# A gated DeltaNet's chunk preparation by pairs of directions, with inverse steps on 32 new rows and beta inside the block inverses

## The chip, the cores and the metric

The kernel runs on one core of one Trainium2 chip. The metric is device time in microseconds (us) of one execution. Three runs of the kernel before the change took 1604.45, 1605.53 and 1607.15 us, a median of 1605.53. A separate execution was recorded by the hardware profiler. Engines: TensorE (PE, with PEld for its weight loads), VectorE (DVE), ScalarE (ACT), GpSimd (POOL) and SyncE (SP, which here issues nearly all DMAs).

## The reference

One layer of a diffusion backbone over 1024 latent and 256 context tokens of width 1024: adaptive normalisation, one input projection, two groups of heads (a gated DeltaNet with 4 heads of 128, and neighbourhood attention with 8 heads of 64), an output projection and a SwiGLU network. The change touches only what the DeltaNet computes for each chunk ahead of its scan. Cut to that:

```python
def chunk_gated_delta_rule(q, k, v, g, beta, S0):
    gam = jnp.cumsum(g..., axis=-1)                       # log decay, per chunk
    decay = jnp.exp(jnp.where(tril, gam[..., :, None] - gam[..., None, :], -jnp.inf))
    kb = k * beta[..., None]
    m = jnp.where(strict, einsum("bhncd,bhnmd->bhncm", kb, k) * decay, 0.0)
    a_mat = jnp.eye(CHUNK) + m
    u = triangular_solve(a_mat, v * beta[..., None], lower=True, unit_diagonal=True)
    w = triangular_solve(a_mat, kb * jnp.exp(gam)[..., None], lower=True, unit_diagonal=True)
    qk = jnp.where(tril, einsum("bhncd,bhnmd->bhncm", q, k) * decay, 0.0)
    ...                                                   # then a scan over the chunks
o_f, S_f = chunk_gated_delta_rule(q, k, v, g[0], beta[0], S0_f)
o_b, S_b = chunk_gated_delta_rule(rev(q), rev(k), rev(v), rev(g[1]), rev(beta[1]), S0_b)
```

So for each chunk, head and direction the inverse of a unit triangular matrix is needed, and the masked product of q and k with its decay.

## The kernel before, in words

The kernel works with chunks of 128 tokens: 10 chunks (2 of context, 8 latent), 4 heads, 2 directions d, so 20 cases (d, c). It runs in stages.

1. Modulation and normalisation, then the projection (L970 to L1045). Its work is a list of jobs: blocks of 128 columns (`Block`, kinds k, q, v, nk, nq) and row tiles (`Wide`, kinds z and nv). Each product is done in three parts, high times high, low times high and high times low, all from L397 or L580.
2. Beside the projection, `Background` generators put other work between its products. `bg` holds first `block_inverses` (L781), which inverts the 32x32 diagonal blocks of all 80 matrices, and then `preps` (L870), which makes the 128x128 inverses. `bg2` holds the sums of the modulation. Between two k steps of a block `bg.step` advances that work, by 1 step up to the job number `turn` and by 3 after it (L1030); between row tiles by 2 and by 5 (L1022, L1024). Latent chunks can only be prepared when the q blocks are done. What is left is drained ahead of the last block, nq 3 (L999).
3. The scan over the chunks in both directions (L1112), with neighbourhood attention (L247) put between its products, then the output projection and the SwiGLU network.

The order that each engine's queue has in the end is made by a scheduler in the language's tile layer, by its own costs and the dependencies; it moves instructions against the order in which the code issues them.

Preparation of one case (`prep`, L896): POOL makes two tiles `rg` (L903), ACT and POOL lay the 32x32 blocks from the DMA tile `xc` on the diagonals of `fx` and `x0` (L908, L909). PE sums the decays (L913, L914), ACT takes the exponential (L917), DVE multiplies `kk` by it and by -beta, head by head (L919), and for latent chunks `at` by the exponential (L923). PE multiplies by the diagonal blocks (L928), ACT copies that to `f` (L930). Three steps then extend the inverse from the diagonal: PE multiplies all 128 rows by `f` (L937) and DVE adds `x0` (L938). Up to three cases are alive at once, each one stage further at a time, and the products go through two PSUM banks named `pr`. SP loads `kk`, `xc` and `at` (L888, L889, L893), and stores `y` and `am` through the list `stores` (L947). After the last case the attention's pool takes over the memory, and its loads (L253 to L276) follow on SP.

`block_inverses` ends by writing U and its blockwise transpose to `x_d` (L858 to L864).

Of the kernel before, what the change touches and what calls it, by code (L numbers as in the profile page):

```python
# [9 lines left out]
F32 = mybir.dt.float32  # L10
F32R = mybir.dt.float32r
# [3 lines left out]
OP = mybir.AluOpType  # L15
# [72 lines left out]
def hybrid(ctx, tc, a, dbg):  # L88
# [280 lines left out]
    with ExitStack() as bs:  # L369
# [411 lines left out]
        def block_inverses():  # L781
            with ExitStack() as gs:
# [75 lines left out]
                for d in range(2):  # L858
                    ud = U[:, d * NU:(d + 1) * NU]
                    ut = g4.tile([128, NU, 32], F32, name="ut", tag="ut")  # L860
                    dve.transpose(fl(ut), fl(ud))
# [8 lines left out]
        def preps():  # L870

            first_half.close()
            with ExitStack() as gs:
                pk = pools(gs, "pk", "left")
                shift(gs, "ppad", "left", 64)
                pp = pools(gs, "pp", "left")

                def work(name, bufs=2, dt=F32):
                    return (pk if name == "kk" else pp).tile([128, 4, 128], dt, name=name, tag=name, bufs=bufs)

                x0s, fxs = [[work(f"{m}{i}", 1) for i in range(k)] for m, k in (("x0", 3), ("fx", 2))]
                for t in x0s + fxs:
                    pool.memset(t, 0.0)

                def fetch(d, c):

                    kk, xc = work("kk", 4), pp.tile([128, 2, 4, 32], F32, name="xc", tag="xc", bufs=2)
                    sp.dma_start(kk, kk_d[:, c])  # L888
                    sp.dma_start(xc, x_d[:, d, :, c * 4:c * 4 + 4])  # L889
                    at = None  # L890
                    if c >= 2:
                        at = work("at", 2)
                        sp.dma_start(at, qk_d[:, c - 2])  # L893
                    return d, c, kk, xc, at

                def prep(n, d, c, kk, xc, at):  # L896
                    lat = c >= 2
                    mle = M[C_LE + d].rearrange("p (o i) -> p o i", o=1).to_broadcast([128, 4, 128])
                    rgs = []
                    for gg in (GH, GL):  # L900
                        rg = work("rg", 2, F32R)
                        src = gg.bitcast(F32)[:, d, c].rearrange("p (h o) -> p h o", o=1).to_broadcast([128, 4, 128])
                        pool.tensor_tensor(rg, src, mle, OP.mult)  # L903
                        rgs.append(rg)
                    x0, fx = x0s[n % 3], fxs[n % 2]
                    for b in range(4):
                        q = slice(b * 32, b * 32 + 32)
                        act.copy(fx[q, :, q], xc[q, 1])  # L908
                        pool.tensor_copy(x0[q, :, q], xc[q, 0])  # L909
                    yield 1  # L910
                    p = bank("pr")
                    for j, rg in enumerate(rgs):
                        pe.matmul(p, mr[:, d], fl(rg), start=j == 0, stop=False)  # L913
                    pe.matmul(p, mr[:, 4], mneg[:, d].rearrange("p (o i) -> p o i", o=1).to_broadcast([128, 4, 128]),  # L914
                              start=False, stop=True)
                    e = work("y", 4)
                    act.activation(fl(e), p, AF.Exp)  # L917
                    for h in range(4):
                        dve.scalar_tensor_tensor(kk[:, h], kk[:, h], NB[:, d, c, h:h + 1], e[:, h],  # L919
                                                 op0=OP.mult, op1=OP.mult)  # L920
# [5 lines left out]
                    p = bank("pr")  # L926
                    for h in range(4):
                        pe.matmul(p[:, hs[h]], kk[:, h], fx[:, h], start=True, stop=True)  # L928
                    f = kk
                    act.copy(fl(f), p)  # L930
                    yield 1
                    y = e
                    src = x0
                    for _ in range(3):
                        p = bank("pr")
                        for h in range(4):
                            pe.matmul(p[:, hs[h]], f[:, h], src[:, h], start=True, stop=True)  # L937
                        dve.tensor_tensor(fl(y), p, fl(x0), OP.add)  # L938
                        src = y
                        yield 1  # L940
                    stores.append((y_d[d, c], y, tick[0] + 2))

                stores, tick = [], [0]

                def flush(n):
                    while stores and stores[0][2] <= n:
                        sp.dma_start(*stores.pop(0)[:2])  # L947

                todo = [(d, ORDER[d][i]) for i in range(NCH) for d in range(2)]
                live, landing = [], []  # L950
                n = 0
                while live or todo or landing:
                    if not landing and todo and (todo[0][1] < 2 or all(x in done for x in queries)):
                        landing.append(fetch(*todo.pop(0)))
# [5 lines left out]
                    nxt = []  # L960
                    for g in live:
                        tick[0] += 1
                        flush(tick[0])
                        if next(g, 0):
                            nxt.append(g)
                        yield
                    live = nxt
                flush(tick[0] + 2)

        jobs = first + [Block("k", 2), Block("k", 3), Wide("z", 1, zp)]  # L970
# [717 lines left out]
```

## Time and profile before

| what | us |
| --- | --- |
| runs, median (lowest to highest) | 1605.53 (1604.45 to 1607.15) |
| span of the profiled execution, first to last instruction | 1601.8 |
| PE busy in it | 1509.9 (94%) |
| DVE busy | 1038.7 (65%) |
| ACT busy | 706.1 (44%) |
| POOL busy | 205.5 (13%) |
| preparation's first and last step products (L937) | 294.5 and 588.9 |
| first score product of the attention (L296) | 623.8 |

The span is the only time that the profile gives for its own execution; the median of the runs is 3.7 us above it. Lines such as L937 are lines of the kernel's file. A group's row gives line, engine, operation, `output<-inputs`, shapes and count, then busy us and the mean ns of one, then the engine's idle time before them and who ended it. Products are pipelined and their ends are modelled: a product's price is best read from the time between two starts. An fp32 product appears as two instructions on PE, each with its own weight load. Releasers are inferred from semaphore events.

### The profile page before, as it was taken

To read this page: it belongs to the slowest core of one execution; us is meant where nothing else is said; L and a number is where in the kernel's file an instruction comes from. 1 tells how busy PE (TensorE), PEld (TensorE's weight loads), DVE (VectorE), ACT (ScalarE), POOL (GpSimd) and SP (SyncE) were. 2 spreads that over 40 slices of the span, in tenths; PEclk is the share of its full clock that TensorE was granted. 3 is DMA by queue.
4 is the path that set the end of the run, shared out by engine and by line. 5 is a ranking of instruction groups with operands and counts; after the bars stand their busy time and mean duration, and the time that the engine had idled before them with its cause. 6 is when DMAs were issued, how large, how long until landed. Compare 5 with 4: busy or idle time off the path is not lost. (4 is left out here: it accounts for less than half of the span.)

```text
span 1601.8 us, 24051 instructions
## 1 busy us (share of the span) xinstructions
PE 1509.9 (94%) x8626; PEld 1269.3 (79%) x8626; DVE 1038.7 (65%) x1934; ACT 706.1 (44%) x1341; POOL 205.5 (13%) x277
## 2 busy tenths in 40 slices
PE   4999999899898897999899999999999999999999
PEld 2788787679788786788777887888888888888887
DVE  4774496674364476667898648956665655679652
ACT  5342554553332325666674347333333333545441
POOL 0054401611333320011110000000000000000000
PEclk8999999999999999999999999999999999999999
DMA  9254222665345538999754910522333333698742
GB/s 387 63 190 133 71 74 78 202 200 178 117 150 184 182 102 228 311 286 288 217 161 135 310 55 27 197 99 99 112 101 107 116 109 109 233 369 299 254 153 85
DMA packets 206407, 271.03 MB, mean 169 GB/s; under 512 B 15952, under 2 KB 115792, under 8 KB 205264
## 3 DMA queue, kind: packets, MB, share of 16 engines
q1 hardware_dynamic: 200816, 264.73, 50.8%
q10 hardware_dynamic: 5472, 4.76, 0.9%
q8 instruction: 68, 1.11, 0.3%
q14 instruction: 51, 0.42, 0.1%
HBM read 204.68 MB, written 68.94 MB: 171 GB/s over the span
## 5 line engine op out<-in xcount | busy, mean ns | idle before, releaser
L397 PE MATMUL blk<-hh,whi 128*128 128x512 f32 (+1 forms) x416 | 125.1, 393 | 4.2 <-ACT hh L702 2.8
L1325 ACT CAST uhi<-ws 128x512 fp32r<-128x512 f32 x91 | 54.7, 622 | 153.8 <-PE ps L1264 75.1
L1325 ACT CAST uhi<-wq 128x512 fp32r<-128x512 f32 x101 | 60.3, 621 | 135.7 <-issue 61.3
L397 PE MATMUL blk<-hh,wlo 128*128 128x512 f32 (+1 forms) x416 | 117.8, 375 | 0.6 <-POOL wlo L194 0.6
L397 PE MATMUL blk<-hl,whi 128*128 128x512 f32 (+1 forms) x416 | 117.5, 374 | 0.0
L1326 DVE TENSOR_TENSOR ulo<-wq,uhi 128x512 fp32r<-128x512 f32 x101 | 67.2, 686 | 66.3 <-ACT uhi L1325 35.4
L1264 PE MATMUL ps<-hT,uhi 128*128 128x512 f32 x336 | 103.9, 390 | 3.1 <-ACT hT L1439 3.1
L1264 PE MATMUL ps<-lT,uhi 128*128 128x512 f32 x336 | 103.9, 391 | 0.0
L1264 PE MATMUL ps<-hT,ulo 128*128 128x512 f32 x336 | 103.8, 390 | 0.0
L1264 PE MATMUL ps<-hB,uhi 128*128 128x512 f32 x288 | 89.7, 392 | 0.0
L1264 PE MATMUL ps<-lB,uhi 128*128 128x512 f32 x288 | 89.2, 391 | 0.0
L1264 PE MATMUL ps<-hB,ulo 128*128 128x512 f32 x288 | 88.9, 389 | 0.0
L397 PEld LDWEIGHTS blk<-hh,whi 128*128 128x128 f32 x416 | 70.8, 194 | 19.7 <-issue 4.9
L397 PEld LDWEIGHTS blk<-hl,whi 128*128 128x128 f32 x416 | 73.5, 192 | 15.2 <-issue 1.7
L397 PEld LDWEIGHTS blk<-hh,wlo 128*128 128x128 f32 x416 | 73.3, 191 | 15.2 <-POOL wlo L194 0.9
L1326 DVE TENSOR_TENSOR ulo<-ws,uhi 128x512 fp32r<-128x512 f32 x91 | 60.7, 685 | 37.7 <-ACT uhi L1325 29.4
L580 PE MATMUL blk<-zhi,hh 128*128 128x256 f32 (+1 forms) x288 | 84.4, 293 | 0.0
L580 PE MATMUL blk<-zhi,hl 128*128 128x256 f32 (+1 forms) x288 | 82.9, 288 | 0.0
L580 PE MATMUL blk<-zlo,hh 128*128 128x256 f32 (+1 forms) x288 | 82.2, 285 | 0.0
L193 ACT CAST whi<-wraw 128x1024 fp32r<-128x1024 f32 x26 | 27.3, 1048 | 112.7 <-PE blk L397 55.7
L1264 PEld LDWEIGHTS ps<-hT,uhi 128*128 128x128 f32 x336 | 62.8, 188 | 16.5 <-ACT hT L1439 3.5
L1264 PEld LDWEIGHTS ps<-hT,ulo 128*128 128x128 f32 x336 | 63.4, 189 | 13.3
(352 smaller groups left out, 3749.0 us busy)
## 6 DMA issues: line engine op xcount, KB each, us to landing
wq<-w_fo SPq DMA_DIRECT2D x99, 256.0 KB
wq<-w_gu SPq DMA_DIRECT2D x88, 256.0 KB
wad<-wa SPq DMA_DIRECT2D x64, 256.0 KB
bt<-rpb SPq DMA_DIRECT2D x64, 192.0 KB
t_d<-g SPq DMA_DIRECT2D x22, 512.0 KB
fr<-t_d SPq DMA_DIRECT2D x44, 256.0 KB
f_d<-g SPq DMA_DIRECT2D x33, 256.0 KB
fr<-f_d SPq DMA_DIRECT2D x33, 256.0 KB
```

Of the source, the lines that this page charges most:

```text
L193: act.copy(h, r)
L397: pe.matmul(o, ww[:, k], xx[k][:, s], start=k == 0 and j == 0, stop=k == KT - 1 and j == 2)
L580: pe.matmul(p[:, :c1 - c0], x[k][:, s], ww[:, k, c0:c1], start=k == 0 and j == 0, stop=k == KT - 1 and j == 2)
L1264: pe.matmul(o, w[wi][:, k], x[xi][:, k], start=first and k == 0 and j == 0, stop=k == n - 1 and j == 2, skip_group_check=True)
L1325: act.copy(hi, self.raw[key])
L1326: dve.tensor_tensor(lo, self.raw[key], hi.bitcast(F32), OP.subtract)
```

## The change

Preparation now takes a pair, both directions of the same step i of the scan order, in one generator, and every stage is issued for d = 0 and d = 1 together.

- `block_inverses` multiplies one of the two stored block forms by NB (which is -beta with the norm of k) on DVE ahead of its store. The diagonal product then carries beta, so the multiplication of `kk` by beta head by head goes, and one elementwise product of 128x512 with the exponential is left.
- The step tile `y` begins with the diagonal blocks. Step n computes only the 32 rows that are new (rows block n for one direction, block 3 - n for the other) over the 32n columns that can be nonzero. The two directions write different groups of 32 PSUM partitions, in two banks, and their products alternate by head. DVE copies the new rows of d = 0, ACT those of d = 1; nothing is added.
- `at` is multiplied in place and stored from there. The tiles' buffer numbers double, six tiles are cleared at the start, not five, and y is stored one tick earlier.
- A second pair may start once the first has passed three stages. The background is advanced by 1 between k steps and by 2 between row tiles, also after `turn`.

The diff:

```diff
@@ block_inverses
                     dve.transpose(fl(ut), fl(ud))
-                    sp.dma_start(x_d[:, d, d], ud)
-                    sp.dma_start(x_d[:, d, 1 - d], ut)
+                    plain, scaled = (ud, ut) if d == 0 else (ut, ud)
+                    sp.dma_start(x_d[:, d, 0], plain)
+                    dve.tensor_tensor(scaled, scaled, NB[:, d].rearrange("p c (h o) -> p (c h) o", o=1).to_broadcast(
+                        [128, NU, 32]), OP.mult)
+                    sp.dma_start(x_d[:, d, 1], scaled)
@@ preps
-                x0s, fxs = [[work(f"{m}{i}", 1) for i in range(k)] for m, k in (("x0", 3), ("fx", 2))]
-                for t in x0s + fxs:
+                fxs = [work(f"fx{d}", 1) for d in range(2)]
+                ys = [[work(f"y{d}{i}", 1) for d in range(2)] for i in range(2)]
+                for t in fxs + ys[0] + ys[1]:
                     pool.memset(t, 0.0)
+                q32 = [slice(b * 32, b * 32 + 32) for b in range(4)]
...
-                def prep(n, d, c, kk, xc, at):
...
+                def prep(i, got):
+                    y = ys[i % 2]
                     rgs = []
...
+                    for d, c, kk, xc, at in got:
+                        for q in q32:
+                            act.copy(fxs[d][q, :, q], xc[q, 1])
                     yield 1
...
-                    for h in range(4):
-                        dve.scalar_tensor_tensor(kk[:, h], kk[:, h], NB[:, d, c, h:h + 1], e[:, h],
-                                                 op0=OP.mult, op1=OP.mult)
-                    if lat:
-                        am = work("am", 3)
-                        dve.tensor_tensor(am, at, e, OP.mult)
-                        stores.append((at_d[d, c - 2], am, tick[0] + 2))
+                    for (d, c, kk, xc, at), e in zip(got, es):
+                        dve.tensor_tensor(kk, kk, e, OP.mult)
+                    for (d, c, kk, xc, at), e in zip(got, es):
+                        for q in q32:
+                            pool.tensor_copy(y[d][q, :, q], xc[q, 0])
+                        if at is not None:
+                            dve.tensor_tensor(at, at, e, OP.mult)
+                            stores.append((at_d[d, c - 2], at, tick[0] + 2))
                     yield 1
...
-                    for _ in range(3):
-                        p = bank("pr")
-                        for h in range(4):
-                            pe.matmul(p[:, hs[h]], f[:, h], src[:, h], start=True, stop=True)
-                        dve.tensor_tensor(fl(y), p, fl(x0), OP.add)
-                        src = y
+                    for n in range(1, 4):
+                        blk = (q32[3 - n], q32[n])
+                        cols = (slice(128 - 32 * n, 128), slice(0, 32 * n))
+                        ps = [bank("pr").rearrange("p (h i) -> p h i", h=4) for _ in got]
+                        for h in range(4):
+                            for (d, c, kk, xc, at), p in zip(got, ps):
+                                pe.matmul(p[blk[d], h, :32 * n], kk[:, h, blk[d]], y[d][:, h, cols[d]],
+                                          start=True, stop=True)
+                        dve.tensor_copy(y[0][blk[0], :, cols[0]], ps[0][blk[0], :, :32 * n])
+                        act.copy(y[1][blk[1], :, cols[1]], ps[1][blk[1], :, :32 * n])
                         yield 1
-                    stores.append((y_d[d, c], y, tick[0] + 2))
+                    for d, c, kk, xc, at in got:
+                        stores.append((y_d[d, c], y[d], tick[0] + 1))
...
-                    if landing and len(live) < 3:
-                        live.append(prep(n, *landing.pop(0)))
-                        n += 1
+                    if landing and (not live or len(live) < 2 and live[0][1] >= 3):
+                        live.append([prep(*landing.pop(0)), 0])
@@ the projection's loop
-                        bg.step(5)
+                        bg.step(2)
...
-                    bg.step(1 if n < turn else 3)
+                    bg.step(1)
```

More of the change, by code (lines that the diff above doesn't have):

```diff
@@ new lines, in preps, with fetch @@
+                q32 = [slice(b * 32, b * 32 + 32) for b in range(4)]
+                def fetch(i):
+                    got = []
+                    for d in range(2):
+                        c = ORDER[d][i]
+                        kk, xc = work("kk", 6), pp.tile([128, 2, 4, 32], F32, name="xc", tag="xc", bufs=4)
+                        sp.dma_start(kk, kk_d[:, c])
+                        sp.dma_start(xc, x_d[:, d, :, c * 4:c * 4 + 4])
+                        at = None
+                        if c >= 2:
+                            at = work("at", 4)
+                            sp.dma_start(at, qk_d[:, c - 2])
+                        got.append((d, c, kk, xc, at))
+                    return i, got
@@ new lines, in prep @@
+                def prep(i, got):
+                    y = ys[i % 2]
+                    rgs = []
+                    for d, c, kk, xc, at in got:
+                        mle = M[C_LE + d].rearrange("p (o i) -> p o i", o=1).to_broadcast([128, 4, 128])
+                        for gg in (GH, GL):
+                            rg = work("rg", 4, F32R)
+                            g = gg.bitcast(F32)[:, d, c].rearrange("p (h o) -> p h o", o=1).to_broadcast([128, 4, 128])
+                            pool.tensor_tensor(rg, g, mle, OP.mult)
+                            rgs.append(rg)
+                    for d, c, kk, xc, at in got:
+                        for q in q32:
+                            act.copy(fxs[d][q, :, q], xc[q, 1])
+                    yield 1
+                    es = []
+                    for d, c, kk, xc, at in got:
+                        p = bank("pr")
+                        for j in range(2):
+                            pe.matmul(p, mr[:, d], fl(rgs[2 * d + j]), start=j == 0, stop=False)
+                        pe.matmul(p, mr[:, 4], mneg[:, d].rearrange("p (o i) -> p o i", o=1).to_broadcast(
+                            [128, 4, 128]), start=False, stop=True)
+                        e = work("e", 2)
+                        act.activation(fl(e), p, AF.Exp)
+                        es.append(e)
+                    for (d, c, kk, xc, at), e in zip(got, es):
[6 more added lines that the diff above has]
+                            stores.append((at_d[d, c - 2], at, tick[0] + 2))
+                    yield 1
+                    ps = []
+                    for d, c, kk, xc, at in got:
@@ L935, in prep @@
                         p = bank("pr")
                         for h in range(4):
-                            pe.matmul(p[:, hs[h]], f[:, h], src[:, h], start=True, stop=True)
-                        dve.tensor_tensor(fl(y), p, fl(x0), OP.add)
-                        src = y
+                            pe.matmul(p[:, hs[h]], kk[:, h], fxs[d][:, h], start=True, stop=True)
+                        ps.append(p)
+                    for (d, c, kk, xc, at), p in zip(got, ps):
+                        act.copy(fl(kk), p)
@@ L947, in flush @@
                         sp.dma_start(*stores.pop(0)[:2])
-                todo = [(d, ORDER[d][i]) for i in range(NCH) for d in range(2)]
+                todo = list(range(NCH))
                 live, landing = [], []
-                n = 0
                 while live or todo or landing:
-                    if not landing and todo and (todo[0][1] < 2 or all(x in done for x in queries)):
-                        landing.append(fetch(*todo.pop(0)))
-                    if landing and len(live) < 3:
-                        live.append(prep(n, *landing.pop(0)))
-                        n += 1
+                    if not landing and todo and (todo[0] < 2 or all(x in done for x in queries)):
+                        landing.append(fetch(todo.pop(0)))
+                    if landing and (not live or len(live) < 2 and live[0][1] >= 3):
+                        live.append([prep(*landing.pop(0)), 0])
                     if not live:
                         yield
-                    nxt = []
-                    for g in live:
+                    for g in list(live):
                         tick[0] += 1
                         flush(tick[0])
-                        if next(g, 0):
-                            nxt.append(g)
+                        g[1] += 1
+                        if not next(g[0], 0):
+                            live.remove(g)
                         yield
-                    live = nxt
                 flush(tick[0] + 2)
```

37 lines of the change are left out of this document (3 added, 34 removed).

## Prediction

> **What bounds the kernel now.** I read the page first, then the busy time by stage, then TensorE's own groups, waits and timeline in the stage that the change touches, and last the queue rows around that stage's end.
>
> ```profile
> span 1601.8 us, 24051 instructions
> PE 1509.9 (94%) x8626; PEld 1269.3 (79%) x8626; DVE 1038.7 (65%) x1934; ACT 706.1 (44%) x1341; POOL 205.5 (13%) x277
> ```
>
> TensorE is busy 94% of the span, so whatever leaves its queue shortens the kernel unless a wait takes its place. The columns of the next view are the stretch in us, its length, busy us of PE, PEld, DVE, ACT and POOL, the granted TensorE clock, and DMA.
>
> ```profile
> core 0: us, PE busy (x) PEld busy (x) DVE busy (x) ACT busy (x) POOL busy (x), PEclk, DMA share, GB/s
> 280.00:312.00 32.00, 28.18 (x152) 21.81 (x151) 24.14 (x34) 16.93 (x33) 20.46 (x31) 0.95 0.68 214
> 312.00:440.00 128.00, 120.32 (x743) 104.85 (x742) 66.13 (x89) 56.41 (x90) 33.82 (x29) 0.99 0.52 164
> 440.00:592.00 152.00, 137.36 (x934) 125.64 (x933) 84.18 (x136) 45.84 (x99) 47.44 (x79) 0.94 0.47 152
> 592.00:621.00 29.00, 27.39 (x140) 22.13 (x139) 22.39 (x29) 7.51 (x11) 2.47 (x5) 1.00 0.83 217
> ```
>
> The first stretch prepares the four context chunks, the third nearly all latent ones, beside the block products of the projection. In the third PE bounds (137 of 152 us) while DVE has 84, ACT 46 and POOL 47. Its clock is the lowest, 0.94. What preparation itself takes from PE:
>
> ```profile
> L937 PE MATMUL pr<-y,kk 128*128 128x128 f32 x320 | 43.7, 286 | 3.4 <-ACT kk L930 2.6 <-DVE y L938 0.8
> L928 PE MATMUL pr<-fx,kk 128*128 128x128 f32 x160 | 28.8, 317 | 18.3 <-DVE y L938 7.2 <-DVE kk L919 6.9 <-issue 3.5
> L937 PE MATMUL pr<-x,kk 128*128 128x128 f32 x160 | 22.9, 288 | 1.8 <-ACT kk L930 1.2 <-ACT y L917 0.5
> ```
>
> **The change, part by part.**
>
> **The steps on 32 new rows.** L937 is 480 instructions (320 + 160; one product is two). Busy times overlap, so I price by starts:
>
> ```profile
> 444.27 1.95 PE L937 MATMUL pr<-y,kk 128*128 128x128 f32 x16
> 445.97 0.83 PE L397 MATMUL blk<-hh,whi 128*128 128x256 f32 x3
> ...
> 447.81 1.05 PE L937 MATMUL pr<-y,kk 128*128 128x128 f32 x8
> 448.62 0.60 PE L397 MATMUL blk<-hh,whi 128*128 128x256 f32 x2
> ```
>
> Sixteen take 1.70 us and eight take 0.81, so 0.104 us each: 480 x 0.104 = 50 us. The changed kernel still issues 480 (10 pairs x 3 steps x 2 directions x 4 heads x 2), but of 32, 64 and 96 columns with 32 columns of weights, on two column strips. By columns, one strip after the other, a pair costs 16 x 0.104 x (0.25 + 0.5 + 0.75) = 2.5 us, all ten 25 us. Two strips at once is a form that the trace has elsewhere:
>
> ```profile
> 657.64 0.32 PE L318 MATMUL sc<-pt,vc 128*64 128x128 f32 x1
> 657.65 0.32 PE L318 MATMUL sc<-pt,vw 128*64 128x128 f32 x1
> 657.80 0.27 PE L318 MATMUL sc<-pt,vc 128*64 128x128 f32 x1
> ...
> 657.91 0.27 PE L318 MATMUL sc<-pt,vc 128*64 128x128 f32 x1
> ...
> 658.88 0.49 PE L1132 MATMUL ps<-s,qT 128*128 128x128 f32 x2
> ```
>
> Two instructions of different strips start 0.01 us apart, and pairs every 0.11, the price of one full-width instruction: strips overlap. The ten pairs take 658.88 - 657.64 = 1.24 us, so 0.14 over 10 x 0.11 is for going into the strip form and out again. Ten pairs x 3 steps x 0.14 = 4 us. In the built order of the changed kernel 166 of the 240 products alternate strips and 74 stand in runs of one strip: 0.7 x 12.5 + 0.3 x 25 + 4 = 20 us. The shortest interval per instruction that the rows show is 0.055 us (two in 0.11); as a floor it would give 480 x 0.055 + 4 = 30. Columns alone and full overlap give 12.5 + 4 = 17. I take 23, near the first, since the smallest form (32 columns) is shown nowhere. **Gain 27 us, ends 20 and 33.**
>
> **Waits before preparation.** What PE waited for in this stage, us in total, times, longest, in the four largest rows; below them the clock in the stretches after two such waits:
>
> ```profile
> PE pr L928 <- DVE y L938: 7.2, 4, 4.0
> PE pr L928 <- DVE kk L919: 6.9, 11, 2.1
> PE pr L937 <- ACT kk L930: 3.8, 2, 2.6
> PE pr L928 <- issue: 3.5, 1, 3.5
> ```
>
> ```profile
> 517.90:524.70 6.80, 5.93 (x25) 5.67 (x26) 4.09 (x10) 2.37 (x6) 2.66 (x3) 0.50 0.42 130
> 534.90:538.20 3.30, 3.10 (x14) 3.10 (x15) 0.74 (x2) 0.94 (x3) 0.00 (x0) 0.50 0.42 162
> ```
>
> They make 21 us, and after them the clock is halved. Clocks of 0.95, 0.99 and 0.94 over 32, 128 and 152 us are 1.6 + 1.3 + 9.1 = 12 us of full-speed time, some of it inside the waits. At most 33 can go; none need. Three things work on it. The scaling by beta leaves the chain:
>
> ```profile
> L919 DVE SCALAR_TENSOR_TENSOR kk<-kk,NB,y 128x128 f32<-128x128 f32 x80 | 41.6, 576 | 47.7 <-ACT y L917 47.5
> L938 DVE TENSOR_TENSOR y<-pr,x 128x512 f32<-128x512 f32 x60 | 40.9, 687 | 40.0 <-PE pr L937 36.4 <-DMA y_d<-y 2.0 <-issue 1.0
> L453 DVE SCALAR_TENSOR_TENSOR cacc<-cr,cw,cacc 128x1022 f32<-128x1022 f32 (+3 forms) x48 | 51.5, 1085 | 0.7
> ```
>
> Four operations of 576 ns (2.3 us) between the exponential and L928 become one 128x512 product, about 0.69 by L938's size. Sixty additions of 687 ns become 30 copies on DVE and 30 on ACT, of 32 partitions and at most 384 elements, shorter than 687 each. And the pace falls from three steps per k (five per tile) to one (two), each for two directions: 100 visits of PE to preparation become 50, and in the built order most visits have seven to fifteen block products between them. What stays is DVE's queue: runs of L453 (1.09 us each) still stand ahead of some copies, and now ACT must be done too. Everything in PE's queue behind such a product, so the projection itself, waits with it. I take 20 of 33, as the kk row and about two thirds of the rest. **Gain 20, ends 0 and 33.**
>
> **The start.** U is scaled by NB before its second store: two 128x1280 products on DVE. L861 on the same shape takes 1.5 us (277.35 below). POOL clears six tiles, not five, and makes four rg before the first exponential group can end, not two:
>
> ```profile
> 277.35 1.50 DVE L861 STREAM_TRANSPOSE ut<-WK 128x1280 f32<-128x1280 f32 x1
> ...
> 285.24 0.98 POOL L883 MEMSET fx<- 128x512 f32 x2
> 286.20 1.03 POOL L903 TENSOR_TENSOR rg<-GH,cst 128x512 fp32r<-128x512 f32 x1
> ```
>
> The scaled store, which the memory of preparation waits for, is 1.5 us later, one memset is 0.5 (two take 0.98), two rg are 2.1: 4 us in which PE stands at its first rg, as its order puts them at the same place as before. **Loss 4, ends 0 and 6** (0 if the block products ahead of it run late).
>
> **The end.** The slower pace leaves the last two inverse steps of the last pair to the last block, nq 3.
>
> ```profile
> 589.97 0.32 SPq L947 DMA_DIRECT2D y_d<-y  x1
> 590.34 0.42 SPq L253 DMA_DIRECT2D qs<-nq_d  x1
> ...
> 597.38 0.59 SPq L276 DMA_DIRECT2D vc<-nv_d  x1
> ...
> 616.68 0.36 SPq L527 DMA_DIRECT2D v_d<-vt  x1
> ```
>
> Attention's first loads follow the last y store now. In the changed order of SP they follow that store and also v 2's store (616.68 here), so they move some 27 us towards the scores, whose first product is at 623.78:
>
> ```profile
> 623.78 0.27 PE L296 MATMUL sc<-kh,qs 128*128 128x256 f16 x1 [0.78 <-ACT cr L485]
> ```
>
> The loads to vc take 7 us to issue (590.34 to 597.38), the first bias follows: about 625 to 627 in place of 623.8, a loss of 2. The heads of the next head pair, loaded early before, then compete with the scan's loads: estimate 2 more. **Loss 4, ends 0 and 12** (12: the last stretch moves 29 us x 217 GB/s = 6.3 MB; half of it moved later is 14 us of transfer, nearly all uncovered).
>
> **At nothing:** the same numbers of loads and stores (kk, xc, at, y_d, at_d), the products with 128 columns (L928) and the three 512-column ones, the in-place product of at. DVE and POOL fall by removed work, with 84 and 47 of 152 us busy there; if that cover were gone, a copy of at most 0.69 us would lie open per step, 30 x 0.69 = 21 us, which is inside the waits' ends.
>
> **Sum:** 27 + 20 - 4 - 4 = 39 us off the profiled execution's 1601.8, so 1562.8. The median of the runs, 1605.5, is 3.7 above that span; I keep the 3.7: **1566**.
>
> **A rule against it.** The strips overlap only if the next weights load while products stream:
>
> ```profile
> L318 PEld LDWEIGHTS sc<-pt,vw x384: 132/137/232, 636.0 to 860.9; 128*64 128x64 f32 x192
> L937 PEld LDWEIGHTS pr<-y,kk x320: 186/192/333, 299.0 to 588.8; 128*128 128x128 f32 x160
> ```
>
> 64 columns more cost 55 ns, so 32 columns some 27 ns; in L318 two loads of 64 columns fit in the 0.11 us of a pair without lengthening it. The Trainium skill, "TensorE: Matmul & The Clock Gate", Part 3, says that a weight load overlaps products in flight only when its row group differs; both strips here use all 128 rows. By that rule the loads would stand in line, the gain of this part would be 8 us and not 27, and the time 1585; the L318 rows disagree with it.
>
> **The rivals.**
>
> *Only the streaming is gained.* Waits move from the additions to the copies behind the runs of L453, now on two engines, and stay 33 us. For it: the largest wait is on DVE's queue, not on PE. Against: half the visits. 27 - 8 = 19 us: 1586.
>
> *The strips do not overlap and the loads stand open.* 25 us by columns, 480 x 0.027 = 13 of loads, 4 of changes: 42 us for 50. Gain 8 + 20 - 8 = 20: 1585. Against it the L318 rows.
>
> *The waits go wholly.* The gain is 30 + 33 - 6 = 57: 1548. For it: the wide spacing of the visits.
>
> *Slower: two engines at each step.* Each of 50 visits needs both banks of pr free, so both engines' evacuation. All old waits then go (33) with the 19 of above, 52 us in all; the kernel is slower once the mean new wait passes 52/50 = 1.04 us. At 1.3 us, a third of the largest wait shown (4.0), the loss is 65: 13 us slower, 1618. Against it: the two engines are half idle, and mean waits now are 21 us over 100 visits.
>
> **How the numbers follow.** A measurement can tell about 0.2%, 3 us. Forecast 0.50, streaming only 0.18, strips apart 0.06, all waits gone 0.20, slower 0.06. The forecast's own range is 1555 to 1577. The range 1540 to 1588 takes in 1548, 1585 and 1586; slower and the outer halves of the others stay out. Faster 0.92, same 0.02, slower 0.06.
>
> **What would show it.** The step's products, priced by starts, at 0.7 to 0.8 us per pair and step, strips 0.01 us apart; PE's waits on pr near 10 us and the clock of that stage above 0.96; the stage from 280 to the first score (343.8 us) at about 305; PE waiting for rg near 287 for some 4 us; the first attention load just behind v 2's store. The prediction is wrong if waits on the copies of y reach the old 21 us, or if scores wait for their heads or biases by more than some us.

## The result and the profile after

The changed kernel takes 1580.8 us (median of four runs, 1576.8 to 1583.3) against 1605.8 for the kernel before (four runs): ratio 0.9839, 95% interval 0.9824 to 0.9854. The prediction was 1566 us, range 1540 to 1588: the direction and the range hold, the size is 15 us too large. The profiled execution has a span of 1575.0 us against 1601.8, so 26.8 us go where 39 were forecast; it is the shortest of the four runs, 4 us below their median.

First the page's span and busy row of the changed kernel, then its busy time by the first three of the same stages (columns as before: PE, PEld, DVE, ACT, POOL, granted clock, DMA share, GB/s). Lines of the stages behind preparation have moved down by 15, so the first product of the output projection is L1256 (L1241 before).

```profile
span 1575.0 us, 23911 instructions
PE 1476.1 (94%) x8626; PEld 1230.5 (78%) x8626; DVE 997.3 (63%) x1846; ACT 719.8 (46%) x1373; POOL 224.4 (14%) x278
```

```profile
280.00:312.00 32.00, 28.84 (x177) 20.77 (x175) 20.68 (x21) 19.68 (x39) 26.74 (x35) 0.89 0.61 195
312.00:440.00 128.00, 122.78 (x792) 107.16 (x790) 60.62 (x74) 58.87 (x94) 44.14 (x34) 0.97 0.59 185
440.00:592.00 152.00, 132.00 (x1015) 110.28 (x1015) 74.80 (x106) 68.08 (x136) 52.20 (x75) 0.96 0.52 167
```

The scores now begin inside the third stretch, at 585.9 us. The steps' products in TensorE's timeline, each with the row behind it:

```profile
425.81 0.45 PE L953 MATMUL pr<-y,kk 128*32 128x32 f32 x16
426.18 0.86 PE L397 MATMUL blk<-hh,whi 128*128 128x256 f32 x3
...
429.88 0.64 PE L953 MATMUL pr<-y,kk 128*32 128x64 f32 x16
430.45 0.85 PE L397 MATMUL blk<-hh,whi 128*128 128x256 f32 x3
...
435.53 0.85 PE L953 MATMUL pr<-y,kk 128*32 128x96 f32 x16
436.31 0.39 PE L580 MATMUL blk<-zhi,hh 128*128 128x256 f32 x1
```

By the starts, a pair's three steps take 0.37 + 0.57 + 0.78 = 1.72 us where they took 3 x 1.70 = 5.1. What PE waited for from 270 to 620 us (total, times, longest):

```profile
PE pr L953 <- DVE y L955: 6.2, 3, 3.5
PE sc L296 <- DMA vw<-vw_d: 4.4, 1, 4.4
PE pr L942 <- DVE kk L930: 3.8, 2, 3.5
PE pr L953 <- ACT y L956: 3.4, 2, 2.1
PE pr L923 <- POOL rg L913: 2.8, 3, 1.8
...
PE pr L953 <- ACT e L927: 1.7, 1, 1.7
PE sc L296 <- DMA kh<-nk_d: 1.6, 1, 1.6
PE pr L942 <- DVE y L955: 1.6, 1, 1.6
```

The waits on pr are 19.5 us; the kernel before has 25.3. The end of the stage, on SP's queue and then on PE:

```profile
561.55 14.36 SPq L965 DMA_DIRECT2D y_d<-y  x4
577.95 0.37 SPq L527 DMA_DIRECT2D v_d<-vt  x1
578.37 2.10 SPq L253 DMA_DIRECT2D qs<-nq_d  x1
```

```profile
585.91 0.38 PE L296 MATMUL sc<-kh,qs 128*128 128x256 f16 x2 [1.62 <-DMA kh<-nk_d]
...
592.12 0.37 PE L296 MATMUL sc<-kh,qs 128*128 128x256 f16 x1 [4.38 <-DMA vw<-vw_d]
```

SP stands 14.36 us in the last four y stores: the last pair's last step starts only at 573.7 and its y is copied after that. Behind them come v 2's store and attention's first loads, 7.5 us ahead of the first score; before, they had 33. The row that ends the next stage, the first product of the output projection (its start is the first number behind the durations), of the kernel before and of the changed one:

```profile
L1241 PE MATMUL ps<-na,whi x32: 389/389/467, 863.7 to 874.0; 128*128 128x512 f32 x32
```

```profile
L1256 PE MATMUL ps<-na,whi x32: 389/389/467, 837.1 to 847.4; 128*128 128x512 f32 x32
```

So the time moved in two pieces. From 280 us to the first score: 343.8 us before, 305.9 after, **37.9 less**. From the first score to the output projection, the stage of attention and scan that the change does not touch: 863.7 - 623.8 = 239.9 before, 837.1 - 585.9 = 251.2 after, **11.3 more**. What is left runs as before (738.1 and 737.9 us).

The first piece can also be read over the same work, from the same projection product near 280 us to the last one, 1951 and 1950 instructions of PE (columns as above; the kernel before first):

```profile
280.61:618.54 337.93, 310.93 (x1951) 272.81 (x1949) 194.63 (x281) 124.32 (x227) 104.18 (x142) 0.96 0.54 166
```

```profile
280.49:579.82 299.33, 278.00 (x1950) 234.99 (x1949) 150.63 (x192) 138.04 (x259) 123.09 (x143) 0.96 0.54 174
```

Of 38.6 us, 32.9 are PE's busy time and 5.7 its idle time; the granted clock is 0.96 in both.

### The profile page after: what moved, and what is told of

Its sections match the earlier page's. It is cut to its first block, busy times and chain, and to the rows that moved or that the text cites. A ratio compares the mean times of both kernels' runs of the same rounds, so it can differ in the third digit from the quotient of the medians.

```text
span 1575.0 us, 23911 instructions
## 1 busy us (share of the span) xinstructions
PE 1476.1 (94%) x8626; PEld 1230.5 (78%) x8626; DVE 997.3 (63%) x1846; ACT 719.8 (46%) x1373; POOL 224.4 (14%) x278
## 5 line engine op out<-in xcount | busy, mean ns | idle before, releaser
L194 POOL TENSOR_TENSOR wlo<-wraw,whi 128x1024 fp32r<-128x1024 f32 x18 | 45.0, 2501 | 202.7 <-ACT whi L193 189.1
L1279 PEld LDWEIGHTS ps<-lT,uhi 128*128 128x128 f32 x336 | 63.3, 189 | 13.3
```

Of the source, the lines that this page charges most:

```text
L194: lo_engine.tensor_tensor(o, r, h.bitcast(F32), OP.subtract)
L1279: pe.matmul(o, w[wi][:, k], x[xi][:, k], start=first and k == 0 and j == 0, stop=k == n - 1 and j == 2, skip_group_check=True)
```

## The experiments

Each stands against the kernel before, run beside it on the same chip; times are medians, and each kernel is the changed one with the edit shown, unless said otherwise. "Preparation stage" is from 280 us to the first score, "scan stage" from there to the first output-projection product. The kernel before took 1605.7 to 1606.2 us beside them. The changed kernel's four runs lie 6.5 us apart, so stage times, which come from one profiled execution each, need not add up to the differences of the medians within a few us.

**The steps at full width**

```diff
-pe.matmul(p[blk[d], h, :32 * n], kk[:, h, blk[d]], y[d][:, h, cols[d]],
+pe.matmul(p[:, h], kk[:, h], y[d][:, h],
...
-dve.tensor_copy(y[0][blk[0], :, cols[0]], ps[0][blk[0], :, :32 * n])
+dve.tensor_copy(y[0][blk[0], :, cols[0]], ps[0][blk[0], :, cols[0]])
```

> The changed kernel with one thing undone on TensorE: each step multiplies all 128 columns of weights by all 128 columns of y, as the kernel before did, and the same 32 new rows are copied out by the same two engines. Pairs, pace, copies, loads, stores and the folded beta stay. The streaming theory of the prediction: 480 instructions cost about 50 us again in place of 18 to 20, so the time rises by 27 to 32 us over the changed kernel's 1580.8, to 1605 to 1613, and the sixteen products of a step take about 1.7 us. Rival (only streaming is not what was gained; the waits fell by the pace and the pairs): the products fill gaps in which PE would have waited anyway, and the time rises by less than 15 us, to under 1596.

1607.0 us (ratio 1.0012, 0.9997 to 1.0027): 26.2 more than the changed kernel, and no faster than the kernel before. All else in the change adds up to nothing measurable without the narrow products, but it is not nothing in each stage. In its profiled execution (1613.5 us) the preparation stage takes 334.1 us, 28.2 more than in the changed kernel and 9.7 less than before; the scan stage takes 259.1, 19.2 more than before. In its timeline a step takes the old 1.70 us:

```profile
439.92 1.95 PE L953 MATMUL pr<-y,kk 128*128 128x128 f32 x16
441.62 0.82 PE L397 MATMUL blk<-hh,whi 128*128 128x256 f32 x3
```

**One strip after the other**

```diff
-for h in range(4):
-    for (d, c, kk, xc, at), p in zip(got, ps):
+for (d, c, kk, xc, at), p in zip(got, ps):
+    for h in range(4):
         pe.matmul(p[blk[d], h, :32 * n], kk[:, h, blk[d]], y[d][:, h, cols[d]],
```

> The changed kernel with each step's eight products of one strip before the eight of the other, so that strips do not overlap; amount and forms of the products are the same. Theory of full overlap: eight of one strip take what sixteen of alternating strips take now (0.38, 0.57 and 0.78 us by the width), so eight pairs whose products alternate now cost 1.73 us more each: 10 to 14 us more, 1591 to 1595, and sixteen take 0.75, 1.1 and 1.5 us. The rule of the Trainium skill that only another row group lets weight loads overlap ("TensorE: Matmul & The Clock Gate", Part 3) expects no difference: within 2 us of 1580.8.

1580.4 us (0.9852, 0.9831 to 0.9874): no change, so my 10 to 14 us are wrong. The side that expected no difference has the time right, but not the mechanism, for the strips do overlap:

```profile
424.56 0.59 PE L953 MATMUL pr<-y,kk 128*32 128x32 f32 x16
425.08 0.85 PE L397 MATMUL blk<-hh,whi 128*128 128x256 f32 x3
...
428.78 0.89 PE L953 MATMUL pr<-y,kk 128*32 128x64 f32 x16
429.60 0.85 PE L397 MATMUL blk<-hh,whi 128*128 128x256 f32 x3
...
434.68 1.21 PE L953 MATMUL pr<-y,kk 128*32 128x96 f32 x16
435.82 0.39 PE L580 MATMUL blk<-zhi,hh 128*128 128x256 f32 x1
```

Sixteen take 0.52, 0.82 and 1.14 us: more than alternating (0.37, 0.57, 0.78, which is also what eight of one strip take where they stand alone in the changed kernel), less than twice that. In the built order these steps have eight and eight; in the records the second strip's first product starts when five of the first strip's eight have started, so the strips overlap by half even in this order. The three steps of a pair cost 0.76 us more, some 5 us in the seven pairs whose products all alternated; at the edge of what the interval can tell.

**Beta outside the block inverses**

```diff
-dve.tensor_tensor(scaled, scaled, NB[:, d].rearrange("p c (h o) -> p (c h) o", o=1).to_broadcast(
-    [128, NU, 32]), OP.mult)
...
-dve.tensor_tensor(kk, kk, e, OP.mult)
+for h in range(4):
+    dve.scalar_tensor_tensor(kk[:, h], kk[:, h], NB[:, d, c, h:h + 1], e[:, h],
+                             op0=OP.mult, op1=OP.mult)
```

> The changed kernel with beta taken out of the block inverses again: U is stored unscaled, and the exponential is multiplied into kk by four operations per direction with NB, as in the kernel before, in place of one. All else as changed. Prediction's theory (the four operations stood in the chain to the first product and made a third of the waits): PE's waits for kk rise from 3.8 us to 10 or more, DVE takes 10 pairs x 2 x 1.6 = 32 us more, and the time rises by 6 to 15 us. Rival (the visits are spaced so widely that 1.6 us more of DVE per direction is hidden): the waits for kk stay under 7 us, and the time within 3 us of 1580.8; at the start it gains up to 1.5 us, since the scaling before x_d's store goes.

1588.5 us (0.9901, 0.9884 to 0.9918): 7.7 more, inside the 6 to 15 of the theory. But its reason fails: PE waits 3.9 us for kk, not 10, and its waits on pr are 19.3 us in all, as in the changed kernel. DVE is busy for 1006.8 us against 997.3, 9.5 more and not 32. Over the same products as above:

```profile
279.90:588.92 309.02, 286.47 (x1950) 240.78 (x1949) 162.09 (x251) 137.88 (x259) 115.90 (x143) 0.94 0.52 167
```

Of 9.7 us more, 8.5 are PE's busy time, at a clock of 0.94 against 0.96: 309 x 0.02 = 6 us of full-speed time. Why the clock is lower is open. Folding beta is worth about 8 us; that it is worth them through the waits for kk is not shown.

**Clearing y later.** The four clears of y are moved on POOL behind the rg of the pair that first uses them.

```diff
-for t in fxs + ys[0] + ys[1]:
+for t in fxs:
     pool.memset(t, 0.0)
...
     rgs.append(rg)
+if i < 2:
+    for t in y:
+        pool.memset(t, 0.0)
```

> The changed kernel with the four clears of y on POOL moved behind the first pair's and the second pair's four rg. Prediction's theory of the start: PE's waits for rg (2.8 us in three waits from 286 to 291) go, and the halved clock that follows them with it: 2 to 4 us faster than the changed kernel. Rival: the first pair's four rg are 4 us of POOL in themselves, the clears wait behind them and the copies of y behind the clears, and PE waits for these in place of rg: within 1 us of the changed kernel, with waits on y from POOL.

1582.1 us (0.9853, 0.9839 to 0.9866): no gain. The first rg product starts 1 us sooner, at 287.05, but PE waits 3.5 us for rg where it waited 2.8. The rival's waits on y from POOL do not appear. The built order has eight fewer instructions of PE ahead of this group, so it stands waiting sooner, and four rg one after another (1.0 us each at the shortest) set the spacing of these products in any case.

**The pace, three ways.** First only in the wide tiles:

```diff
 if n >= turn:
-    bg.step(2)
+    bg.step(3)
```

> The changed kernel with only the pace in wide tiles raised, three visits in place of two. Preparation ends about one block earlier: one query load of attention stands ahead of the second v store, the others follow it, and the w_out loads stay behind all heads' loads, as in the changed kernel. Theory T splits here: if the heads' first loads are the cost, the stretch from the first score to the first output-projection product falls from 251.2 to about 245; if the w_out casts in the busy part of the scan are the cost, it stays at 249 to 252. The waits on pr stay near 19 us in either case. Rival L expects 249 to 252 in this and in the faster pace alike.

1573.3 us (0.9789, 0.9775 to 0.9802): 7.5 less than the changed kernel. The preparation stage is 312.7 us, 6.8 longer, with waits on pr of 23.2 us where I expected 19; the scan stage is 835.4 - 592.7 = 242.7, 8.5 shorter. The twenty us from the first score on, of the kernel before, the changed one and this one:

```profile
623.80:643.80 20.00, 13.86 (x110) 11.19 (x110) 10.66 (x25) 13.00 (x24) 1.48 (x4) 0.83 0.89 263
```

```profile
585.90:605.90 20.00, 11.54 (x69) 7.99 (x69) 9.17 (x23) 7.93 (x15) 0.62 (x2) 0.66 1.03 317
```

```profile
592.70:612.70 20.00, 13.85 (x113) 10.74 (x113) 10.38 (x28) 12.23 (x24) 1.54 (x4) 0.83 0.84 250
```

The last step's products start some 12 us earlier (561.6 for 573.7), and the scan begins as it did before the change (113 products for 69, clock 0.83 for 0.66). The w_out loads still stand late here, so most of the 11 us goes with the heads' loads and the biases behind them, which this run does not separate. Then also in the blocks:

```diff
-    bg.step(2)
+    bg.step(3)
...
-bg.step(1)
+bg.step(1 if n < turn else 1 + k % 2)
```

> The changed kernel with the pace raised after the turn: blocks advance preparation by one and two visits alternately in place of one, wide tiles by three in place of two. Preparation then ends before block nq 3, and in the built order of SP three of attention's first query loads stand ahead of v 1's store, and the first w_out loads ahead of v 3's store, as in the kernel before. Theory T (the late end of preparation costs the scan stage its 11 us: its first loads and the w_out loads and casts fall into the busy part): the stretch from the first score to the first output-projection product falls from 251.2 us to 240 to 243, the time by 7 to 10 us below the changed kernel's. Rival W (the slower pace is what took the waits away): the waits on pr rise by 6 us or more from 19.5, and the time stays within 3 us of the changed kernel's. Rival L (the scan stage is longer for another reason, such as the lower clock at its start): the stretch stays above 248.

1579.0 us (0.9832, 0.9819 to 0.9846). Both the theory and rival W hold in part: the scan stage is 241.7, with the w_out loads early too, 1 us below the run above; and the waits on pr rise to 26.4. One of them is 12.4 us, at 546.64, for POOL's copy of the diagonal blocks. What stood ahead of that, on SP and then on POOL:

```profile
514.37 18.05 SPq L1056 DMA_DIRECT2D vw_d<-nv_d  x10
532.52 2.93 SPq L965 DMA_DIRECT2D at_d<-at  x2
535.50 1.23 SPq L965 DMA_DIRECT2D y_d<-y  x2
```

```profile
545.32 2.65 POOL L933 COPY y<-xc 32x128 f32<-32x128 f32 x8 [22.57 <-DMA y_d<-y]
```

Ten copies from nv_d to vw_d keep SP for 18 us; the y store waits behind them, and with two sets of y POOL cannot refill the tile until that store has landed.

Last, the kernel before with a slower pace and nothing else of the change:

```diff
-bg.step(5)
+bg.step(4)
...
-bg.step(1 if n < turn else 3)
+bg.step(1 if n < turn else 2)
```

> The kernel before, with only its pace lowered after the turn: blocks advance preparation by two steps per k in place of three, wide tiles by four in place of five. Preparation then ends behind v 2's store, as in the changed kernel, and the w_out loads but one stand behind the heads' loads. Theory T: the stretch from the first score to the first output-projection product rises from 239.9 us to 247 to 252, without any of the change's other parts. Rival L: it stays at 239 to 242. Waits on pr: 25.3 us before; a slower pace should take some of them away, down to 15 to 22 if pace alone thins them, and leave them near 25 if the chain from the exponential to the first product is what they come from. The time then lies between 1598 and 1614.

1618.3 us (1.0078, 1.0064 to 1.0091), 4 us above the largest time expected. Its scan stage is 878.4 - 631.8 = 246.6 us, 6.7 more than before, and its first scores wait like those of the changed kernel, and longer:

```profile
PE sc L296 <- DMA kh<-nk_d: 5.7, 1, 5.7
PE sc L296 <- DMA vw<-vw_d: 4.7, 1, 4.7
```

So the late end alone costs in a kernel without pairs and strips, too. Its preparation stage is 351.8 us, 8.0 longer, and the waits on pr are 27.9 us against 25.3: a slower pace alone takes none away. My reading that visits further apart thin the waits fails here.

**Three sets of y, with the faster pace**

```diff
 (the pace of the second of the three runs above)
-ys = [[work(f"y{d}{i}", 1) for d in range(2)] for i in range(2)]
-for t in fxs + ys[0] + ys[1]:
+ys = [[work(f"y{d}{i}", 1) for d in range(2)] for i in range(3)]
+for t in fxs + ys[0] + ys[1] + ys[2]:
...
-kk, xc = work("kk", 6), pp.tile([128, 2, 4, 32], F32, name="xc", tag="xc", bufs=4)
+kk, xc = work("kk", 4), pp.tile([128, 2, 4, 32], F32, name="xc", tag="xc", bufs=4)
...
-y = ys[i % 2]
+y = ys[i % 3]
```

> The faster pace of e1_pace (one and two visits alternately per k, three per tile) with three sets of y tiles in place of two, and four kk tiles in place of six to make room. In e1_pace POOL's copy of the diagonal blocks stood 22.6 us behind a store of y, which SP could not issue because ten copies from nv_d to vw_d kept SP for 18 us, and PE waited 12.4 us for it. Theory: a third set takes this wait away without any other wait in its place; the stretch from the first score to the first output-projection product stays near 242 us: 8 to 12 us faster than e1_pace's 1579.0, at 1567 to 1571. Rival (fewer kk tiles or the next store bring another wait of the same size): within 4 us of 1579.

1560.2 us (0.9721, 0.9703 to 0.9738), the fastest of all: 20.6 below the changed kernel and 45.9 below the one before. The 12.4 us are gone, waits on y copies total 4.8 us, and the scan stage is 242.7 us. Against the same pace with two sets it is 18.8 us faster, where I expected 8 to 12, so more than that one wait went. Its busy time in the last stage of the projection:

```profile
440.00:572.00 132.00, 127.51 (x1005) 108.43 (x1005) 72.31 (x96) 54.82 (x117) 49.35 (x66) 1.00 0.62 198
```

PE is busy for 127.5 of the last 132 us at full clock, against 132.0 of 152 at 0.96 (6 of these lie behind the first score). With waits on pr of 13.4 us this is near the signs that the prediction named for the change itself (near 10 us, a clock above 0.96).

**The third set at the old pace.** The edit above without its change of pace.

> The changed kernel at its own pace, with three sets of y tiles in place of two and four kk tiles in place of six: e9_y3 without the faster pace. If the buffers of y are what the waits before preparation came from in the changed kernel too (a pair's diagonal copies stand behind the store of the pair before the last), PE's waits on y fall from 11.2 us (6.2 + 3.4 + 1.6) to under 5, and the time falls by 5 to 12 us, to 1569 to 1576, with the stretch from the first score to the first output-projection product still near 251. Rival (these waits stand behind other work of DVE and ACT, runs of the convolution among it, and the third set only paid with the faster pace): waits on y stay at 9 us or more, the time within 4 us of 1580.8.

1576.7 us (0.9823, 0.9806 to 0.9840), 4 less, its interval overlapping the changed kernel's. The waits on y do not fall (6.9 + 3.5 + 2.7 = 13.1 us for 11.2) and the scan stage stays long (255.6). The two kk tiles fewer bring no wait either (3.9 us for kk, 3.8 with six). The rival holds: at the old pace the y store was not what PE waited for. DVE's own timeline in the changed kernel shows what was:

```profile
541.96 8.70 DVE L453 SCALAR_TENSOR_TENSOR cacc<-cr,cw,cacc 128x254 f32<-128x254 f32 x8
550.70 0.29 DVE L955 COPY y<-pr 32x128 f32<-32x128 f32 x1
```

PE's product at 551.13 waited 3.47 us for that 0.29 us copy, which stood behind eight operations of the convolution.

**Both copies on ACT**

```diff
-dve.tensor_copy(y[0][blk[0], :, cols[0]], ps[0][blk[0], :, :32 * n])
+act.copy(y[0][blk[0], :, cols[0]], ps[0][blk[0], :, :32 * n])
```

> The changed kernel with both directions' copies of the new rows on ACT, in place of one on DVE and one on ACT. Theory of two engines (a step waits for the later of two queues): waits on the copies of y (6.2 from DVE, 3.4 from ACT, 1.6 from DVE at the first product) fall to 6 or less, since only one queue has to be free, and the time falls by 4 to 8 us. Rival (DVE is merely what ended last; the wait is for the chain, whose second copy now follows the first on one engine): waits on y from ACT rise to 10 us or more, and the time stays within 4 us of 1580.8 or rises.

1568.0 us (0.9755, 0.9734 to 0.9776): 12.8 less, more than the theory's 4 to 8. The waits on y fall from 11.2 to 8.2, all of them now from ACT; the theory had 6 or less, the rival 10 or more:

```profile
PE pr L953 <- ACT y L956: 5.1, 2, 3.4
...
PE pr L923 <- ACT y L955: 3.1, 2, 2.0
```

The clock of the first two stretches is 0.95 and 0.99 for 0.89 and 0.97, 32 x 0.06 + 128 x 0.02 = 4.5 us. Over the same products as above the stage takes 294.2 us for 299.3, 5.1 less, and the spans of the two profiled executions, 1575.0 and 1567.6, lie 7.4 apart. That the gain comes from leaving DVE's queue fits this, but only 3 us of it stand in the list of waits.

**Two further combinations.** e9_y3 with two visits per k in every block after the turn:

> e9_y3 with a still faster pace: two visits per k in every block after the turn, three per tile. Theory from e9_y3 (with three sets of y no store stands in the way, so visits may come closer): the waits stay near 16 us in total, the scan stage near 242 us, and the time stays at 1558 to 1563, no gain left in the end. Rival (visits closer together take back the waits that the wide spacing hid): waits before preparation rise by 6 us or more, 1566 or above.

1564.7 us (0.9738, 0.9724 to 0.9751), 4.5 above e9_y3, with intervals that just overlap: waits on pr are 18 us for 13, the scan stage 242.6 as there. A faster pace gains nothing more at the end, and visits closer together seem to cost. And e9_y3 with both copies on ACT:

> e9_y3 (faster pace, three sets of y) with both directions' copies on ACT. If the two gains are of different things (e7_act: the visits' queue, 12.8 us; e9_y3: the end of the stage and the buffers, 20.6 us), they add in part: 1548 to 1555, with the waits on y (4.8 us in e9_y3) under 2. Rival (both took the same waits before the steps): within 3 us of e9_y3's 1560.2, with ACT's copies in place of DVE's in the list of waits.

1570.3 us (0.9776, 0.9761 to 0.9791): 10 us *slower* than e9_y3, so neither the sum nor the rival. The waits on y are 3.4 us, but those for kk on DVE have grown to 9.2 us in five waits (5.6 in e9_y3), and those for kk on ACT to 3.1 (0.6). Why kk comes later on DVE when DVE has less to do is open: every edit of this kind changes the built order on all engines. Not run alone: the pairing of directions, the earlier store of y, and the in-place product of at.

## Why the prediction was right, and where its sizes were off

The direction, the range and the largest term are right. But 1580.8 lies outside the forecast's own range of 1555 to 1577, and nearer to the rival "only the streaming is gained" (1586, chance 0.18) than to 1566. The prediction also named scores that wait for their heads by more than some us as a sign of being wrong, and they wait 6.0.

*Streaming of the steps (27, ends 20 and 33): right.* The rows above give 1.72 us for a pair whose strips alternate, 17 us for all ten if they did; groups whose strips stand apart in the queue bring it to about 20. From 50 that is a gain of 30, and undoing it alone gave back 26.2 in the medians, 28.2 in the preparation stage. The 0.14 us for going into the strip form and out again, taken from L318, came nearly true (0.37 us for eight starts 0.032 apart leave 0.11). The margin that I put on the 32-column form was not needed: an alternating step takes 0.57 us in the mean where I named 0.7 to 0.8. The rival of strips that stand open (1585) is out: a step at 32 columns in 0.37 us cannot hold sixteen loads in line at the 27 ns estimated there.

*Waits before preparation (20, ends 0 and 33): mis-sized, about 6 in its place.* The waits on pr fall from 25.3 to 19.5, by 5.8. The clock, which I had put into the same term, gives nothing: it is 0.96 in both kernels over the same work. The kk row did fall (6.9 to 3.8). What failed is "about two thirds of the rest", and the working was off there too: 20 less the kk row's 6.9 is half of the other 26. A wait of 3.47 us, among the longest, still stands behind a run of L453, as the rival that moves the waits there had it, and e2_slow shows that a slower pace by itself removes nothing. The chain also got shorter by less than I said, 0.9 us a case and not 1.6. The one product in place of four operations (41.6 us for 20 cases, 2.08 each) was priced at 0.69 us from L938, and it takes 1.19:

```profile
L930 DVE TENSOR_TENSOR kk<-kk,e 128x512 f32<-128x512 f32 x20 | 23.5, 1190 | 46.1 <-ACT e L927 46.1
```

The five of the twenty that no record of POOL overlaps take 0.68 to 0.69 us. The other fifteen, most of them beside POOL's rg, take 1.36 in the mean (three of them 0.69 to 0.77). e9_y3 and e7_act show that part of the term was there to be had, by buffers and pace, or by another queue.

*The start (4, ends 0 and 6): about 1 in its place.* PE waits 2.8 us for rg where it waited 1.6. "About 4 us near 287" did not come, and e4_start finds nothing to win from the clears. The clock of that stretch is 0.89 for 0.95, 2 us of full-speed time; over the whole stage it evens out.

*The end (4, ends 0 and 12): the right mechanism, mis-sized; 11.3 in its place.* The first attention load follows v 2's store, as forecast. I priced the first score's delay and some competition; but the heads arrive singly behind 14 us of y stores, the first scores wait 1.6 and 4.4 us, and the clock of the first twenty us is 0.66 in place of 0.83, so 69 products start there in place of 110. e1c_tiles takes 8.5 of the 11.3 away with one digit of pace, though its preparation stage is 6.8 longer, and e2_slow brings 6.7 of it into the kernel before.

The sum: the preparation stage was forecast at about 305 and took 305.9. That is luck in part: a streaming gain 3 too small and a start loss 3 too large met a gain from waits 14 too large. Streaming 30 + waits on pr 5.8 is 36 of the 37.9 measured, and 2 us have no row. The scan stage then lost 7 us more than forecast, and the median lies 5.8 us above the profiled span, not 3.7. The slower rival (two engines at each step, decided at 1.04 us a visit) did not happen: 13 us of waits on the steps and behind them, over 50 visits, are 0.26.

## What to carry to other kernels

When background work is slowed to thin its waits, look at what is queued behind its last store: here the change cost 11 us in a stage that nobody edited, and one digit of the pace gave back most of that, for 6.8 us more in the stage before and 7.5 us less in all. A short copy on a chain takes the length of the queue that it joins, not its own (0.29 us behind 8.7), so count what stands ahead of it on its engine and how many buffers let the next round start. Price narrow matrix products by their starts and add the change of form once per group.

## What the hardware showed that I had not expected

- Strips overlap across the order of the queue. Sixteen products in the order of eight and eight take 0.52, 0.82 and 1.14 us, between the alternating 0.37, 0.57, 0.78 and twice the cost of eight.
- Products of one strip start 32, 56 and 83 ns apart for 32, 64 and 96 columns: 0.86 to 0.88 ns a column for the wider two, 1.0 for the smallest. Their weight loads are recorded at a median 110 ns each:

```profile
L953 PEld LDWEIGHTS pr<-y,kk x480: 106/110/177, 298.8 to 574.2; 128*32 128x32 f32 x160
```

480 x 0.11 = 53 us of loads lie in some 20 us of products, so in the records loads overlap each other as well as the products. That is not special to strips: in the kernel before, loads of 0.19 us stand at one start per 0.104 us.
- An elementwise product on DVE of the same shape takes about twice as long where POOL's records lie beside it: 0.68 to 0.69 us for the five of L930 without, 1.36 us in the mean for the fifteen with. POOL's rg, 1.04 us at the shortest, take up to 1.49 there. What the two engines share is not shown here.
